# A kept TensorE order for one attention layer: later output products, transposes after the value projection, outputs in a projection bank

## The chip, the core and the metric

The kernel runs on one core of one Trainium2 chip. The metric is the device time of one execution in microseconds, as the median of several runs. Before the change the runs took 1037.28, 1037.68 and 1043.04 us; the median is 1037.68 us.

## What is computed

The reference is a decoder layer with three token mixers and a routed mixture of experts, followed by two layers of another design; 256 tokens of 1024 channels pass through all of them. Only the attention of the last layer is touched. Its core:

```python
def moba_attention(h, w_qkv, w_o):
    qkv = (h @ w_qkv).reshape(Bsz, S, 3, N_HEADS, HEAD_DIM)
    q = rope(q, pos) * (HEAD_DIM ** -0.5)
    k = rope(k, pos)
    ...
        s_own = jnp.where(kpos[None, :] <= qpos[:, None], s_own, NEG_INF)
        p = jax.nn.softmax(jnp.concatenate([s_sel, s_own], axis=-1), axis=-1)
    ...
    return o @ w_o
```

With 256 tokens there is a single block of 256 keys, so the selected blocks are all masked and what is left is causal attention of 16 heads of 64 channels over 256 positions, then the projection `w_o` and the residual. A gated feed-forward layer with a short convolution stands before it and another one after it.

## The kernel before

Weights arrive as 1 MB tiles of float32, and each is split into a high part in `float32r` (a ScalarE copy in `split`, L287) and a low part (a VectorE subtraction, L291), so that every product is made of three TensorE matmuls: high by high, high by low, low by high. `unit` (L467) is 48 such matmuls of 256 columns into one PSUM bank; `tm_unit` is the same for two banks with tokens on the partitions; `acc_rows` (L327) is 48 matmuls into four banks that are kept over all calls.

PSUM has eight banks in two rings of four: `bank` (projections: `un`, `pv`, and at the end the four output accumulators `wo`) and `abank` (attention: `sc` for scores, `ptT` for transposed weights, `po` for outputs). Splits rotate over three SBUF tiles, large tiles over eight.

The attention works on four blocks of four heads. For block j, `qkv(j, 0)` and `qkv(j, 1)` make queries and keys (`un`, 48 matmuls each) and rotate them: one VectorE product with the cosines, four on 32 partitions with the sines (`rb`), and a GpSimd addition (L1484). `qkv(j, 2)` makes the values (`pv`, 48 matmuls) and ScalarE evicts them. `scores(j)` makes 16 matmuls of float32 and 8 that add the causal mask, then two maxima for each head on VectorE (L1508, L1509), a scaling, two exponentials for each head on ScalarE with their sums, and one VectorE reciprocal (L1513). `weights(j)` multiplies by the reciprocals (one VectorE instruction over all heads for the first 128 queries, L1520, tile `pe`, and four ScalarE instructions), makes twelve transposes (L1526) into four banks and copies each bank to SBUF, on VectorE for even heads and on ScalarE for odd ones (tile `pT`). `values(j)` makes 16 matmuls into `po`, a ScalarE copy to the high part `oh` and a VectorE subtraction to the low part `ol`. The projection `acc_rows` of block j takes `oh` and `ol` of block j.

The loop at L1551 writes the stages in this order for j from 0 to 3: queries of j, scores of j-1, keys of j, weights of j-1, values projection of j, outputs of j-1. After it stand, for block 3, scores, projection 0, weights, projection 1, outputs, projection 2, and projection 3. This order is only a priority: a list scheduler that plans with a cost model of its own puts the instructions on each engine's queue, taking what it believes to be ready, earlier lines first. On the chip every queue then runs in the planned order. `chain` (L213) can fix that order for TensorE: while `chained[0]` is true, each instruction that `mm` or `flip` makes is ordered behind the one before. In the attention `chained[0]` is false, and the transposes at L1526 don't go through `flip`.

Of the kernel before, what the change touches and what calls it, by code (L numbers as in the profile page):

```python
# [21 lines left out]
P = 128  # L22
# [152 lines left out]
def build(tc, I, out, dbg=None, stop=None):  # L175
    nc = tc.nc
# [11 lines left out]
    def nm(s):  # L188
        uid[0] += 1
        return f"{s}_{uid[0]}"  # L190

    def big(n="b", dt=F32):
        return b8.tile([P, RAW], dt, tag="b8", name=nm(n))

    def mid(n="m", dt=F32, bufs=10):
        return sm.tile([P, 512], dt, tag="t512", name=nm(n), bufs=bufs)

    def tiny(n, w, dt=F32, bufs=2, p=P, tag=None):
        return sm.tile([p, w], dt, tag=tag or f"tn_{n}", name=nm(n), bufs=bufs)

    def bank(n="ps"):
        return ps.tile([P, 512], F32, tag="ps", name=nm(n), bufs=4)

    def abank(n="pa"):
        return ps.tile([P, 512], F32, tag="acc", name=nm(n), bufs=4)
# [5 lines left out]
    chained = [False, None]  # L211

    def chain(i):  # L213

        if chained[0]:
            if chained[1] is not None:
                behind(i, chained[1])
            chained[1] = i

    def mm(o, l, r, start, stop):  # L220
        chain(nc.tensor.matmul(o, l, r, start=start, stop=stop, skip_group_check=True))  # L221

    def flip(o, i):
        chain(nc.tensor.transpose(o, i, ident))
# [7 lines left out]
    def act(o, i, f, **kw):  # L232
        return S.activation(o, i, f, **kw)  # L233
# [20 lines left out]
    def tt(o, a, b, op):  # L254
        V.tensor_tensor(out=o, in0=a, in1=b, op=op)  # L255

    def ts(o, a, s1, op0, s2=None, op1=None):
        if s2 is None:
            V.tensor_scalar(out=o, in0=a, scalar1=s1, scalar2=None, op0=op0)
        else:  # L260
            V.tensor_scalar(out=o, in0=a, scalar1=s1, scalar2=s2, op0=op0, op1=op1)
# [10 lines left out]
    def ld(ap, n=RAW):  # L272
        t = raw.tile([P, RAW], F32, tag="raw", name=nm("raw"))
        nc.sync.dma_start(out=t[:, :n], in_=ap)
        return t
# [11 lines left out]
    def split(ap, n, on=None):  # L287

        hl = spl.tile([P, RAW], F32R, tag="spl", name=nm("spl"))
        hi, lo = hl[:, :PIECE], hl[:, PIECE:]  # L290
        queue(act(hi[:, :n], ap, AF.Copy), (on or V).tensor_tensor(out=lo[:, :n], in0=ap, in1=r32(hi[:, :n]), op=SUB))  # L291
        return hi, lo
# [34 lines left out]
    def acc_rows(t, xs, acc, first, last):  # L327

        w = [split(t[:, j * D:(j + 1) * D], D) for j in range(2)]
        for j, b in [(j, b) for b in range(KC) for j in range(2)] if last else [(j, b) for j in range(2) for b in range(KC)]:  # L330
            (hi, lo), (xh, xl) = w[j], xs[j]
            o = acc[b // 2][:, (b % 2) * T:(b % 2) * T + T]
            c = slice(b * P, b * P + P)
            mm(o, hi[:, c], xh, first and j == 0 and b % 2 == 0, False)
            mm(o, hi[:, c], xl, False, False)
            mm(o, lo[:, c], xh, False, last and j == 1)
# [27 lines left out]
    def C(name, p=P):  # L364
        return cst[:p, CST[name][0]:CST[name][1]]
# [7 lines left out]
    ident, ones = C("ident"), C("ones")  # L373
# [93 lines left out]
    def unit(src, xh, xl, on={}, order=range(KC)):  # L467

        p = bank("un")
        t = ld(src)  # L470
        cm_unit(t, P, 2, xh, xl, lambda b: (p[:, b * T:b * T + T], b == 0), on=on, order=order)
        return p
# [9 lines left out]
    def twice(rb):  # L482
        return rb.unsqueeze(1).to_broadcast([P, 2, T])
# [895 lines left out]
    def residual(x, acc):  # L1379
        for j in range(4):  # L1380
            s = slice(j * 512, j * 512 + 512)
            tt(x[:, s], x[:, s], acc[j], ADD)
# [87 lines left out]
    def qkv(j, i):  # L1470

        if i == 0:
            state[j] = [big("qkv")]
        g = state[j][0]
        if i < 2:
            p = pre.pop(0) if pre else unit(I["w_qkv"][3 * j + i], xh, xl)
            p3 = p.rearrange("p (h t) -> p h t", h=2)
            a, b_ = g[:, i * 512:i * 512 + 512], mid("rb")
            tt(a.rearrange("p (h t) -> p h t", h=2), p3, twice(cosr), MUL)
            for r in range(4):  # L1480
                src, dst = slice(32 * r, 32 * r + 32), slice(32 * (r ^ 1), 32 * (r ^ 1) + 32)
                tt(b_[dst].rearrange("p (h t) -> p h t", h=2), p3[src],
                   sinr[src].unsqueeze(1).to_broadcast([32, 2, T]), MUL)
            G.tensor_tensor(out=a, in0=a, in1=b_, op=ADD)  # L1484
            return
        t = ld(I["w_qkv"][3 * j + 2])
        pv = [bank("pv") for _ in range(2)]
        tm_unit(t, 256, KC, 0, xh, xl, pv, 7)
        for q in range(2):
            act(g[:, 1024 + q * T:1024 + q * T + T], pv[q][:, :T], AF.Copy, scale=rs[:, q:q + 1])  # L1490

    def scores(j):

        g = state[j][0]
        qr, kr = g[:, 0:512], g[:, 512:1024]
        pcs = [abank("sc") for _ in range(4)]
        for q in range(2):
            for h in range(4):
                s, o = slice(64 * (h % 2), 64 * (h % 2) + 64), (h // 2) * T
                mm(pcs[h][:, q * P:q * P + P + q * P], qr[s, o + q * P:o + q * P + P], kr[s, o:o + P + q * P], q == 0, False)  # L1500
        sums = tiny("sums", 8)
        pe = big("pe").rearrange("p (h t) -> p h t", h=4)
        for h in range(4):
            pc = pcs[h]
            mm(pc[:, 0:128], identb, nca, False, True)
            mm(pc[:, 256:384], identb, nca, False, True)
            m = tiny("amx", 2, bufs=4)
            V.tensor_reduce(out=m[:, 0:1], in_=pc[:, 0:128], axis=AX.X, op=MAX)  # L1508
            V.tensor_reduce(out=m[:, 1:2], in_=pc[:, 128:384], axis=AX.X, op=MAX)  # L1509
            ts(m, m, -0.125, MUL)  # L1510
            act(pe[:, h, 0:128], pc[:, 0:128], AF.Exp, scale=0.125, bias=m[:, 0:1], accum_out=sums[:, 2 * h:2 * h + 1])
            act(pe[:, h, 128:384], pc[:, 128:384], AF.Exp, scale=0.125, bias=m[:, 1:2], accum_out=sums[:, 2 * h + 1:2 * h + 2])
        V.reciprocal(sums, sums)  # L1513
        state[j] += [pe, sums]

    def weights(j):

        _, pe, sums = state[j]
        s2 = sums.rearrange("p (h q) -> p h q", q=2)
        tt(pe[:, :, 0:P], pe[:, :, 0:P], s2[:, :, 0:1].to_broadcast([P, 4, P]), MUL)  # L1520
        pTs = []
        for h in range(4):
            act(pe[:, h, P:3 * P], pe[:, h, P:3 * P], AF.Copy, scale=sums[:, 2 * h + 1:2 * h + 2])
            pt = abank("ptT")
            for b in range(3):
                nc.tensor.transpose(pt[:, b * P:b * P + P], pe[:, h, b * P:b * P + P], ident)  # L1526
            pT = mid("pT")
            if h % 2:
                act(pT[:, :384], pt[:, :384], AF.Copy)
            else:  # L1530
                V.tensor_copy(pT[:, :384], pt[:, :384])
            pTs.append(pT)
        state[j].append(pTs)

    def values(j):

        g, pTs = state[j][0], state[j][3]
        v = g[:, 1024:1536]
        po = abank("po")
        for r in range(2):  # L1540
            for i in range(2):
                h, o = 2 * r + i, po[64 * i:64 * i + 64, r * T:r * T + T]
                mm(o, v[:, 64 * h:64 * h + 64], pTs[h][:, 0:256], r == 0, False)
            for i in range(2):
                h, o = 2 * r + i, po[64 * i:64 * i + 64, r * T:r * T + T]
                mm(o[:, P:], v[:, T + 64 * h:T + 64 * h + 64], pTs[h][:, 256:384], False, True)
        s = slice(j * 512, j * 512 + 512)
        act(oh_[:, s], po, AF.Copy)
        tt(ol_[:, s], po, r32(oh_[:, s]), SUB)

    stages = (scores, weights, values)  # L1551
    for j in range(4):
        for i in range(3):
            qkv(j, i)
            if j:
                stages[i](j - 1)
    acc = [bank("wo") for _ in range(4)]
    for j in range(4):
        if j < 3:
            stages[j](3)  # L1560
        xs2 = [(oh_[:, (2 * j + b) * T:(2 * j + b + 1) * T], ol_[:, (2 * j + b) * T:(2 * j + b + 1) * T]) for b in range(2)]
        acc_rows(ld(I["w_ao"][j]), xs2, acc, j == 0, j == 3)
    residual(X, acc)
    dump("a1T", X)
    conv_ffn(1)
# [3 lines left out]
    po = [bank("fo") for _ in range(4)]  # L1569
# [54 lines left out]
```

## Time and profile before

| | us |
|---|---|
| median of three runs | 1037.68 |
| the profiled execution | 1044.24 |
| its span, first to last instruction | 1042.3 |
| TensorE busy | 984.4 |
| VectorE busy | 679.6 |
| ScalarE busy | 493.6 |
| GpSimd busy | 23.5 |

The first queries of the attention that stand inside the loop (block 1) start at 731.0 us of the span, and the last projection ends at 837.9 us. Times inside the span are counted from its first instruction. Busy time of TensorE counts a matmul that is overlapped by the next one, so a share of 94% says only that little idle time is visible. The granted clock is given as a share of the full 2.4 GHz.

### The profile page before, as it was taken

To read this page: it belongs to the slowest core of one execution; us is meant where nothing else is said; L and a number is where in the kernel's file an instruction comes from. 1 tells how busy PE (TensorE), PEld (TensorE's weight loads), DVE (VectorE), ACT (ScalarE), POOL (GpSimd) and SP (SyncE) were. 2 spreads that over 40 slices of the span, in tenths; PEclk is the share of its full clock that TensorE was granted. 3 is DMA by queue.
4 is the path that set the end of the run, shared out by engine and by line. 5 is a ranking of instruction groups with operands and counts; after the bars stand their busy time and mean duration, and the time that the engine had idled before them with its cause. 6 is when DMAs were issued, how large, how long until landed. Compare 5 with 4: busy or idle time off the path is not lost.

```text
span 1042.3 us, 18612 instructions
## 1 busy us (share of the span) xinstructions
PE 984.4 (94%) x7751; PEld 870.1 (83%) x7751; DVE 679.6 (65%) x1201; ACT 493.6 (47%) x776; POOL 23.5 (2%) x24
## 2 busy tenths in 40 slices
PE   6999997999989889999999999999899999999996
PEld 5988995555555439899999999999888999999996
DVE  5985554222233217885888777778987589777775
ACT  5646443222223226644555555555555556555554
POOL 0100000000000000100000000000211000000000
PEclk9999897999999999999999999999999999999998
DMA  8952355999999999555454545554333354544001
GB/s 327 419 222 79 122 221 219 417 380 420 420 420 389 420 416 420 191 172 193 163 190 174 195 170 200 168 199 172 122 122 122 133 192 163 199 165 163 1 1 41
DMA packets 35228, 232.45 MB, mean 223 GB/s; under 512 B 4288, under 2 KB 5056, under 8 KB 8640
## 3 DMA queue, kind: packets, MB, share of 16 engines
q1 hardware_dynamic: 34992, 231.14, 57.8%
q8 instruction: 67, 1.10, 0.4%
q14 instruction: 25, 0.20, 0.1%
q10 hardware_dynamic: 144, 0.02, 0.0%
HBM read 230.09 MB, written 1.05 MB: 222 GB/s over the span
## 4 chain that ended last, share of the span: by engine, by line
PE 53%; DMA 8%; DVE 7%; ACT 1%; issue 1%; POOL 0%; SPq 0%; DVEq 0%; ACTq 0%; POOLq 0%
PE un L221 35%; PE fo L221 11%; DMA mw<-in_w_dn_dram 3%; DMA mw<-in_w_gu_dram 3%; PE wo L221 2%; PE so L221 2%; DVE rb L255 2%; DVE spl L291 2%; DMA raw<-in_w_si_dram 1%; PE pv L221 1%; PE ptT L1526 1%; ACT spl L233 0%; PE po L221 0%; ACT pe L233 0%; PE ssq L221 0%
## 5 line engine op out<-in xcount | busy, mean ns | idle before, releaser
L221 PE MATMUL un<-nh,spl 128*128 128x256 f32 x2176 | 400.5, 284 | 2.8 <-DVE spl L291 2.6
L233 ACT ACTIVATE spl<-raw 128x1024 fp32r<-128x1024 f32 (+3 forms) x241 | 251.4, 1045 | 270.1 <-PE un L221 163.9
L291 DVE TENSOR_TENSOR spl<-raw,spl 128x1024 fp32r<-128x1024 f32 (+3 forms) x238 | 289.9, 1221 | 105.1 <-ACT spl L233 102.2
L221 PEld LDWEIGHTS un<-nh,spl 128*128 128x128 f32 x2176 | 342.9, 192 | 4.2 <-DVE spl L291 3.4
L221 PE MATMUL un<-nl,spl 128*128 128x256 f32 x1088 | 308.6, 284 | 1.9 <-DVE nl L264 1.9
L221 PEld LDWEIGHTS un<-nl,spl 128*128 128x128 f32 x1088 | 209.5, 193 | 2.3 <-DVE nl L264 2.3
L221 PE MATMUL fo<-ah,spl 128*128 128x256 f32 x704 | 130.1, 283 | 0.0
L221 PEld LDWEIGHTS fo<-ah,spl 128*128 128x128 f32 x704 | 111.2, 192 | 0.0
L221 PE MATMUL fo<-al,spl 128*128 128x256 f32 x352 | 99.8, 284 | 0.5 <-DVE al L255 0.4
L221 PE MATMUL pgu<-mw,xs 128*32 128x512 f32 x512 | 68.5, 621 | 8.2 <-DMA mw<-in_w_gu_dram 7.3
L1042 DVE COPY xs<-pgx 128x512 f32<-128x512 f32 x15 | 10.4, 691 | 100.1 <-PE pgx L221 100.1
L264 DVE SCALAR_TENSOR_TENSOR fc<-fz,vec,fc 128x254 f32<-128x254 f32 (+1 forms) x176 | 72.9, 477 | 1.4 <-ACT fc L233 1.4
L221 PEld LDWEIGHTS fo<-al,spl 128*128 128x128 f32 x352 | 67.5, 192 | 1.3 <-DVE al L255 1.3
L221 PEld LDWEIGHTS pgu<-mw,xs 128*32 128x32 f32 x512 | 17.3, 113 | 47.0 <-issue 30.6
L221 PEld LDWEIGHTS h<-pmT,yq 128*128 128x128 f32 x256 | 32.1, 190 | 20.5 <-issue 9.6
L233 ACT ACTIVATE su<-pgu,ws 128x512 f32<-128x512 f32 x8 | 5.5, 686 | 81.4 <-PE pgu L221 81.4
L221 PE MATMUL h<-pmT,yq 128*128 128x256 f32 x256 | 37.2, 292 | 7.2 <-DVE yq L264 3.8
L264 DVE SCALAR_TENSOR_TENSOR yq<-pd,ws,yq 128x512 fp32r<-128x512 f32 x32 | 22.9, 747 | 29.0 <-ACT yq L233 29.0
L255 DVE TENSOR_TENSOR fz<-un,rB 128x512 f32<-128x512 f32 x44 | 30.2, 690 | 16.1 <-PE un L221 16.0
L233 ACT ACTIVATE fc<-fz,vec 128x256 f32<-128x256 f32 x88 | 39.2, 496 | 1.1 <-DVE fz L255 1.1
L233 ACT ACTIVATE yq<-pd,ws 128x512 fp32r<-128x512 f32 x32 | 21.0, 685 | 37.7 <-PE pd L221 37.7
L221 PE MATMUL pd<-mw,sg 128*32 128x512 f32 x288 | 36.0, 596 | 1.1 <-DMA mw<-in_w_dn_dram 0.5
(330 smaller groups left out, 1363.8 us busy)
## 6 DMA issues: line engine op xcount, KB each, us to landing
mw<-in_w_gu_dram SPq DMA_DIRECT2D x64, 1024.0 KB, 15.0
raw<-in_w_fu_dram SPq DMA_DIRECT2D x44, 1024.0 KB, 4.7
mw<-in_w_dn_dram SPq DMA_DIRECT2D x28, 1024.0 KB, 12.5
raw<-in_w_fd_dram SPq DMA_DIRECT2D x22, 1024.0 KB, 4.7
raw<-in_w_si_dram SPq DMA_DIRECT2D x12, 1024.0 KB, 16.8
raw<-in_w_qkv_dram SPq DMA_DIRECT2D x12, 1024.0 KB, 4.7
raw<-in_w_o_dram SPq DMA_DIRECT2D x4, 1024.0 KB, 17.3
mw<-in_w_dn_dram SPq DMA_DIRECT2D x8, 512.0 KB, 14.4
```

The costliest lines, as they stand in the source:

```text
L221: chain(nc.tensor.matmul(o, l, r, start=start, stop=stop, skip_group_check=True))
L233: return S.activation(o, i, f, **kw)
L255: V.tensor_tensor(out=o, in0=a, in1=b, op=op)
L264: return V.scalar_tensor_tensor(out=o, in0=a, scalar=s, in1=b, op0=op0, op1=op1, **kw)
L291: queue(act(hi[:, :n], ap, AF.Copy), (on or V).tensor_tensor(out=lo[:, :n], in0=ap, in1=r32(hi[:, :n]), op=SUB))
L1042: V.tensor_copy(o, pg)
L1526: nc.tensor.transpose(pt[:, b * P:b * P + P], pe[:, h, b * P:b * P + P], ident)
```

## The change

The attention's TensorE instructions are chained, from the value projection of block 0 to the last projection, and the transposes go through `flip` so that they are in the chain. The order of stages is a new one: queries of block j, outputs of j-2, scores of j-1, keys of j, value projection of j, weights of j-1. After the loop stand scores of 3, outputs of 2, projections 0 and 1, weights of 3, projection 2, outputs of 3, projection 3. The tile `po` is taken from the ring `bank` for blocks 0 to 2, and from `abank` for block 3. No instruction is added or taken away on any engine.

```diff
-                nc.tensor.transpose(pt[:, b * P:b * P + P], pe[:, h, b * P:b * P + P], ident)
+                flip(pt[:, b * P:b * P + P], pe[:, h, b * P:b * P + P])
...
-        po = abank("po")
+        po = (abank if j == 3 else bank)("po")
...
-    stages = (scores, weights, values)
+    def at(f, j):
+        if 0 <= j < 4:
+            f(j)
+
+    chained[:] = [True, None]
     for j in range(4):
-        for i in range(3):
-            qkv(j, i)
-            if j:
-                stages[i](j - 1)
+        qkv(j, 0)
+        at(values, j - 2)
+        at(scores, j - 1)
+        qkv(j, 1)
+        qkv(j, 2)
+        at(weights, j - 1)
+    scores(3)
+    values(2)
     acc = [bank("wo") for _ in range(4)]
     for j in range(4):
-        if j < 3:
-            stages[j](3)
+        if j == 2:
+            weights(3)
+        if j == 3:
+            values(3)
         xs2 = [(oh_[:, (2 * j + b) * T:(2 * j + b + 1) * T], ol_[:, (2 * j + b) * T:(2 * j + b + 1) * T]) for b in range(2)]
         acc_rows(ld(I["w_ao"][j]), xs2, acc, j == 0, j == 3)
+    chained[:] = [False, None]
     residual(X, acc)
```

## Rows read from the trace of the kernel before

**Rows 1.** The page, busy time: engine, us, share of the span, instructions.

```profile
PE 984.4 (94%) x7751; PEld 870.1 (83%) x7751; DVE 679.6 (65%) x1201; ACT 493.6 (47%) x776; POOL 23.5 (2%) x24
```

**Rows 2.** Stretches: start:end, us, busy us by engine, granted clock, DMA share, GB/s.

```profile
731.00:757.73 26.73, 23.43 (x197) 21.47 (x197) 25.41 (x43) 14.99 (x33) 6.18 (x4) 1.00 0.32 119
757.73:783.87 26.14, 24.06 (x198) 22.69 (x197) 20.42 (x34) 13.35 (x32) 3.07 (x2) 0.93 0.36 126
783.87:808.39 24.52, 22.50 (x198) 21.23 (x196) 20.35 (x33) 13.23 (x32) 3.06 (x2) 1.00 0.33 125
808.39:837.89 29.50, 29.07 (x248) 27.69 (x247) 17.70 (x32) 15.86 (x38) 0.00 (x0) 1.00 0.40 143
```

**Rows 3.** The chain that ended last, attention: start, us, what it was.

```profile
756.35 1.45 PE po L221 x16
757.80 5.96 PE un L221 x48
```

**Rows 4.** TensorE in order of time: start, us, line, instructions [idle before <-releaser].

```profile
738.16 0.38 PE L221 MATMUL pv<-spl,nh 128*128 128x256 f32 x1 [0.91 <-ACT spl L233]
739.27 1.58 PE L221 MATMUL sc<-qkv 64*128 64x128 f32 x16 [0.73 <-POOL qkv L1484]
...
742.71 0.50 PE L221 MATMUL un<-nh,spl 128*128 128x256 f32 x2 [0.89 <-DVE spl L291]
...
763.68 0.49 PE L221 MATMUL sc<-qkv 64*128 64x128 f32 x4
...
765.62 0.36 PE L221 MATMUL un<-nh,spl 128*128 128x256 f32 x1
...
778.01 1.92 PE L1526 MATMUL ptT<-cst,pe 128*128 128x128 f32 x12 [2.08 <-DVE pe L255]
...
782.42 0.44 PE L221 MATMUL po<-pT,qkv 128*64 128x256 f32 x2
...
804.08 1.50 PE L1526 MATMUL ptT<-cst,pe 128*128 128x128 f32 x12 [2.02 <-DVE pe L255]
805.34 0.36 PE L221 MATMUL pv<-spl,nh 128*128 128x256 f32 x1
...
806.94 1.52 PE L221 MATMUL po<-pT,qkv 128*64 128x256 f32 x16
...
810.39 0.92 PE L221 MATMUL sc<-qkv 64*128 64x128 f32 x4 [0.43 <-DVE ol L255]
...
826.11 0.39 PE L221 MATMUL wo<-oh,spl 128*128 128x256 f32 x1
```

**Rows 5.** Stretches after the two waits of the transposes, columns as in group 2.

```profile
778.00:782.50 4.50, 4.49 (x26) 4.27 (x28) 4.24 (x4) 1.46 (x3) 1.00 (x1) 0.62 0.00 0
804.00:807.00 3.00, 2.92 (x26) 2.81 (x27) 2.97 (x3) 1.29 (x3) 1.07 (x1) 1.00 0.00 0
```

**Rows 6.** VectorE in order of time, columns as in group 4.

```profile
763.78 0.69 DVE L255 TENSOR_TENSOR qkv<-un,rope 128x512 f32<-128x512 f32 x1 [0.56 <-PE un L221]
...
777.17 0.69 DVE L255 TENSOR_TENSOR pe<-pe,sums 128x512 f32<-128x512 f32 x1
777.78 2.30 DVE L291 TENSOR_TENSOR spl<-raw,spl 128x1024 fp32r<-128x1024 f32 x1
780.12 1.02 DVE L1531 COPY pT<-ptT 128x384 f32<-128x384 f32 x2
...
803.86 2.30 DVE L291 TENSOR_TENSOR spl<-raw,spl 128x1024 fp32r<-128x1024 f32 x1
...
825.86 1.23 DVE L291 TENSOR_TENSOR spl<-raw,spl 128x1024 fp32r<-128x1024 f32 x1 [1.65 <-ACT spl L233]
827.00 0.68 DVE L255 TENSOR_TENSOR ol<-po,oh 128x512 fp32r<-128x512 f32 x1
```

**Rows 7.** GpSimd in order of time, columns as in group 4.

```profile
777.22 1.78 POOL L1484 TENSOR_TENSOR qkv<-qkv,rb 128x512 f32<-128x512 f32 x1 [8.43 <-DVE rb L255]
```

**Rows 8.** ScalarE in order of time: the copy of the last block's outputs.

```profile
826.23 0.60 ACT L233 ACTIVATE oh<-po 128x512 fp32r<-128x512 f32 x1 [0.41 <-PE po L221]
```

## The prediction

> **What bounds the kernel now.** The page comes first. TensorE is busy for 94% of the span and VectorE, the next one, for 65% [rows 1], so what the attention can give is TensorE's idle or slow time there, and not more. The stretches by block show how much that is. From the queries of block 1 to the end of the last projection there are four stretches of 26.73, 26.14, 24.52 and 29.50 us [rows 2], together 106.9 us. The work in them follows from the chain and the order of time: 48 matmuls of a projection 5.8 to 5.96 us, 16 output matmuls 1.45 [rows 3], 24 score matmuls from 763.68 to 765.62 = 1.94, twelve transposes from 804.08 to 805.34 = 1.26 [rows 4]. A block of the loop is then 3 x 5.87 + 1.94 + 1.26 + 1.45 = 22.3 us, and the last stretch 4 x 5.87 + 4.65 = 28.1. So 4.4 + 3.8 + 2.2 + 1.4 = 11.8 us of 106.9 are lost, and this is the ceiling of any new order: 1.1% of the kernel.
>
> The rows of TensorE say where they go. Twice the transposes wait for the VectorE multiplication `pe`: 2.08 us before 778.01 and 2.02 us before 804.08 [rows 4]. After the first wait the granted clock averages 0.62 over 4.5 us, after the second it stays at 1.00 [rows 5]; 24 matmuls take 778.01 to 782.42 = 4.41 us there and 804.08 to 806.94 = 2.86 us here [rows 4]. The fall to 1.2 GHz costs 1.55 us. Block 1 loses its time in small pieces, 0.91, 0.73 and 0.89 us [rows 4], while VectorE is busy for 25.41 of 26.73 us [rows 2]: VectorE sets that block. Before the scores of block 3, a bank that `po` holds costs 0.43 us [rows 4].
>
> **The change, part by part.** It adds no instruction and no DMA; it moves work on TensorE, and SP's and GpSimd's queues keep their order. In each of blocks 2 and 3 the planned order already was queries, scores, keys, 36 value matmuls, transposes, 12 value matmuls, outputs [rows 4]. So the change does two things: the 12 value matmuls (1.44 us) go ahead of the transposes, and the outputs (1.45 us) go behind the next queries, ahead of the scores.
>
> *Transposes of blocks 1 and 2.* What is late is VectorE's line of work from the end of the queries: it starts at 763.78 and ends with the multiplication at 777.17 + 0.69 = 777.86 [rows 6], 14.1 us. The new order puts `ol` of an older block (0.68 us [rows 6]) into that line: 14.8 us. TensorE's own work from the end of the queries to the end of the value projection becomes 1.45 + 1.94 + 5.87 + 5.87 = 15.1 us. VectorE is ready 0.3 us earlier, the hand-over takes 778.01 - 777.86 = 0.15 us, and both waits go but for some 0.2 us each: 2.08 + 2.02 - 0.4 = -3.7 us. The bounds: -4.1, and 0 if VectorE's order grows by another split or two. I take the middle line because all its pieces are rows; the margin is a few tenths only.
>
> *The clock.* It fell once behind two equal waits, so it is no sure consequence. With the wait that stood ahead of it gone, I take the fall as gone: -1.55. Bounds: -1.55 and +1.55 (one more).
>
> *Queries of block 3, directly behind transposes.* Their first low part was not needed before 783.87 [rows 2]; VectorE makes it right behind the multiplication, in 2.30 us, beside a GpSimd addition of 1.78 us [rows 6, 7]; the same split is 1.23 us without one [rows 6]. Transposes end 0.15 + 1.26 = 1.41 us behind the multiplication, two matmuls of 0.12 need only the high part, and the third waits for 2.30: about +0.65. Bounds: 0, and 1.9 with a split of 1.23 more ahead of it. In block 1 VectorE has its splits ready before.
>
> *Scores of block 3, directly behind transposes.* They need the four banks that the transposes just filled, and so the four copies `pT`. Before, 12 value matmuls and 16 output matmuls lay between. In both blocks that show it, VectorE runs a split of 2.30 us between multiplication and copies, and then two copies in 1.02 us [rows 6]. If that stays, the copies are done 3.3 us behind the multiplication, the transposes 1.4, and only the first two score matmuls fit between (0.2 us): +1.7 us. If the copies come first it is +0.4 (the last copy alone); with both splits of projection 0 ahead, +2.9. I take 1.7, since the rows show a split there. The 0.43 us of the `po` bank goes, as `po` now lies in the other ring: -0.43. That ring then holds queries, `po`, keys and two value banks in turn, five tenants on four banks, each evicted at least one projection (5.9 us) before its bank is needed again: nothing. If that cover went, the last eviction, `oh` and `ol`, would show: 0.60 + 0.68 [rows 6, 8].
>
> *Outputs of block 3, directly ahead of projection 3.* Before, projection 2 (5.9 us) lay between. Now the first matmul of projection 3 waits for `oh` and the second for `ol`. Before, the projection behind the outputs began at 826.11 [rows 4]; the copy ran 0.60 us from 826.23, and the subtraction of 0.68 us ended at 827.68, behind a split that ended at 827.09 [rows 6, 8]. With VectorE free the subtraction would end at about 827.5: +1.45 us. Bounds: 1.4, and 2.7 with a split of 1.23 in the way [rows 6].
>
> *Block 1.* The four value matmuls that ran in the gaps before the scores and behind them [rows 4] are no longer there to fill them: +0.5; transposes are no longer mixed with value matmuls one by one: -0.3. Together +0.2, bounds 0 and +0.5. The gaps themselves stay, as VectorE makes them.
>
> *Moved transposes and outputs of block 3.* They stand one projection later than before, so what they wait for has 5.9 us of cover more: nothing.
>
> The sum: -3.7 - 1.55 + 0.65 + 1.7 - 0.43 + 1.45 + 0.2 = -1.7 us. The profiled execution took 1044.24 us in all (span 1042.3), so the same execution would take 1042.5. The median of the runs is 6.6 us below the profiled one, and all three lie between 1037.28 and 1043.04; I carry the difference over to the median: 1037.68 - 1.7 = 1036.0 us. All terms at their good ends give -4.1 - 1.55 + 0.4 - 0.43 + 1.4 = -4.3 (1033.4); all at their bad ends, without a new fall of the clock, 0 + 0 + 1.9 + 2.9 - 0.43 + 2.7 + 0.5 = +7.6 (1045.3).
>
> **The rivals.** *New waits eat the rest (same time or a little longer).* The waits of the transposes shrink only by the 1.44 us that go ahead of them, since `ol` and splits lengthen VectorE's line: -2.9 instead of -3.7, the clock stays as it was, and the other terms stand: -2.9 + 3.6 = +0.7, 1038.4 us. For it: VectorE is busy for 20.4 of 26 us in these blocks [rows 2] and its line beats TensorE's by 0.3 us only. Against: every piece of the line has a row.
>
> *VectorE becomes the bound (slower).* Place: the VectorE queue ahead of the multiplication of blocks 1 and 2. If the planner puts the two splits of the next queries (2.30 + 1.23 us [rows 6]) ahead of it there, the transposes wait 3.5 us in each block, not 2.05: +2.9, and with the terms at the ends +3.6, the clock as before: +6.5, 1044.2 us. It decides from a wait of 0.3 us on: (4.1 - 3.6) / 2 is what the two waits may last until the gain is spent, clock left aside. Against it: multiplication stands ahead of the splits in the rows [rows 6], and the value projection gives it more time.
>
> *The clock falls more often (slower).* The new order has waits of 1.7, 1.45 and 0.65 us at places where there was none. If the clock falls behind the two longer ones as it did at 779, and the old fall stays, that is 3 x 1.55 in place of 1 x 1.55: from -1.7 to +2.95, so 1040.6 us. A rule stands on this side: the Trainium skill, "TensorE: Matmul & The Clock Gate", section "A second HAM failure mode: psum-queue depth-cycling", says that frequent short idle pieces between groups of matmuls make the clock go up and down, with a loss at each turn. The trace speaks against it here: block 1 has the most such pieces and a granted clock of 1.00 throughout [rows 2, 4].
>
> *All clean (faster).* Copies and splits fall well, every term at its good end: -4.3, 1033.4 us. Beyond that only the small pieces of block 1 could go; to gain over 1% (10.4 us) nearly all of the 11.8 us would have to.
>
> *The order changes nothing.* As the planned order is close to the new one, the sum could be within a few tenths of zero: 1037.7 us.
>
> **The numbers.** Forecast 0.40; new waits eat the rest 0.20; VectorE the bound 0.12; clock 0.08; all clean 0.13; nothing 0.07. From 1033.4 to 1040.6 lies most of it; the runs before spread over 5.8 us, so the range is 1031 to 1042. It leaves out 0.12 for VectorE as the bound and a little on the good side. A difference of under 1% (10.4 us) is what I can't tell from no change; the ceiling of 11.8 us makes faster 0.04, the worst sum of +7.6 makes slower 0.04, same 0.92.
>
> **What the profile after would show.** Right: the transposes of blocks 1 and 2 stand behind 48 value matmuls with waits under 0.5 us; no half clock near 779; a wait of the scores of block 3 on a `pT` copy, over 1 us; a wait of projection 3 on `oh` or `ol`, about 1.4 us; small waits of block 1 as before. Wrong: waits of the transposes over 1 us, or VectorE running splits ahead of `pe`; no wait at projection 3; a queue of VectorE or ScalarE ordered so differently that the feed-forward layer behind starts otherwise.

## The result: slower by 1.0%

The changed kernel takes 1048.39 us (median of 7 runs, 1047.62 to 1052.34), the kernel before 1037.68 (7 runs, 1035.71 to 1044.12): ratio 1.0103, 95% interval 1.0083 to 1.0122. The prediction said 1036.0 with a range of 1031 to 1042 and gave 0.04 to a loss of over 1%.

The profiled execution took 1048.39 us, with a span of 1046.5. The part ahead of the attention varies from execution to execution by some microseconds: the queries of block 1 begin at 731.00 us in the profile before and at 725.04 here, where the queues ahead are the same. So spans can't be compared, but stretches inside can. From the first queries of block 1 to the first matmul of the next layer the kernel before takes 731.00 to 837.73 = 106.7 us, the changed one 725.04 to 841.85 = 116.8 us: +10.1 us, close to the difference of the medians (10.7).

The stretches by block of the kernel after, from the queries of one block to those of the next, the last one from the scores of block 3 on; columns as in [rows 2]:

```profile
725.04:750.29 25.25, 22.64 (x181) 21.47 (x181) 23.96 (x41) 13.92 (x31) 6.91 (x4) 0.93 0.36 126
750.29:779.02 28.73, 25.19 (x199) 24.02 (x198) 22.47 (x35) 13.75 (x33) 3.88 (x3) 0.88 0.40 138
779.02:806.74 27.72, 24.11 (x199) 22.77 (x198) 20.90 (x34) 13.27 (x32) 3.62 (x2) 0.94 0.29 98
806.74:841.85 35.11, 32.09 (x262) 30.13 (x261) 18.01 (x33) 16.92 (x40) 0.00 (x0) 0.95 0.30 112
```

So one sees where the time went: the two middle blocks take 28.7 and 27.7 us for 22.3 us of work, and the clock is below 1.00 in every stretch, where it was below 1.00 in one [rows 2].

TensorE's longest waits in the same stretch of the kernel after (engine, line and what it waited for: us in total, times, longest):

```profile
PE pv L221 <- DVE spl L291: 7.2, 2, 3.6
PE wo L221 <- DVE ol L255: 2.3, 2, 1.8
PE sc L221 <- POOL qkv L1484: 2.3, 1, 2.3
PE wo L221 <- ACT oh L233: 0.7, 1, 0.7
```

The transposes don't stand in it any more. Their wait of 4.1 us has become 7.2 us of waiting in the middle of the value projection, for a low part of its weights. TensorE in order of time, kernel after (columns as in [rows 4]):

```profile
772.27 0.80 PE L221 MATMUL pv<-spl,nh 128*128 128x256 f32 x2 [3.54 <-DVE spl L291]
...
777.13 0.63 PE L224 MATMUL ptT<-cst,pe 128*128 128x128 f32 x2
...
801.07 0.38 PE L221 MATMUL pv<-spl,nh 128*128 128x256 f32 x1 [3.61 <-DVE spl L291]
...
814.94 0.39 PE L221 MATMUL wo<-oh,spl 128*128 128x256 f32 x1 [1.84 <-DVE ol L255]
...
835.25 0.39 PE L221 MATMUL wo<-oh,spl 128*128 128x256 f32 x1 [0.70 <-ACT oh L233]
836.11 0.38 PE L221 MATMUL wo<-ol,spl 128*128 128x256 f32 x1 [0.47 <-DVE ol L255]
```

What VectorE did meanwhile is the point. Kernel after, block 2:

```profile
766.55 0.20 DVE L1513 RECIPROCAL sums<-sums 128x8 f32<-128x8 f32 x1 [1.75 <-ACT pe L233]
766.86 0.69 DVE L255 TENSOR_TENSOR pe<-pe,sums 128x512 f32<-128x512 f32 x1
767.47 0.68 DVE L255 TENSOR_TENSOR qkv<-un,rope 128x512 f32<-128x512 f32 x1
768.17 2.79 DVE L255 TENSOR_TENSOR rb<-un,rope 32x512 f32<-32x512 f32 x4
770.99 4.58 DVE L291 TENSOR_TENSOR spl<-raw,spl 128x1024 fp32r<-128x1024 f32 x3
```

and the same place in the kernel before:

```profile
772.45 1.23 DVE L291 TENSOR_TENSOR spl<-raw,spl 128x1024 fp32r<-128x1024 f32 x1 [0.89 <-ACT spl L233]
773.59 0.20 DVE L1513 RECIPROCAL sums<-sums 128x8 f32<-128x8 f32 x1
773.70 0.64 DVE L255 TENSOR_TENSOR qkv<-un,rope 128x512 f32<-128x512 f32 x1
774.35 2.79 DVE L255 TENSOR_TENSOR rb<-un,rope 32x512 f32<-32x512 f32 x4
```

Before, the order was second split of the value weights, reciprocal, rotation, and the multiplication `pe` last [rows 6]. After, it is reciprocal, multiplication, rotation, and the split last. The multiplication, which the transposes used to wait for, ends at 767.55, some 3.8 us ahead of the time at which the value projection could have ended without a wait (765.45 + 5.87 = 771.32). The split, which TensorE now needs first, comes behind it. The high part of that split, which ScalarE makes, was ready at 767.47:

```profile
766.38 1.09 ACT L233 ACTIVATE spl<-raw 128x1024 fp32r<-128x1024 f32 x1
```

So it is VectorE's own order that holds the low part back, for 3.5 us.

The half clock (1.2 GHz, a granted clock of 0.50) follows the waits. Windows of the kernel after:

```profile
771.90:778.50 6.60, 6.23 (x29) 6.23 (x30) 4.15 (x4) 1.60 (x3) 1.45 (x1) 0.50 0.70 245
801.00:806.00 5.00, 4.93 (x29) 4.93 (x30) 3.60 (x4) 1.34 (x3) 1.17 (x1) 0.66 0.77 241
814.90:820.00 5.10, 5.06 (x29) 5.06 (x30) 1.23 (x1) 1.55 (x3) 0.00 (x0) 0.67 0.15 31
```

What is left of the value projection behind the wait, and the transposes, take 772.27 to 779.02 = 6.75 us and 801.07 to 806.74 = 5.67 us, against 3.97 us at full clock (run e1 below, 771.49 to 775.46): 2.8 and 1.7 us. The 78 matmuls behind the third wait take 814.94 to 825.89 = 10.95 us, 1.5 us more than at 11.59 us for 96 (run e3). Together 6.0 us.

The account: value projection +7.15, transposes -4.10, clock 6.0 in place of 1.55 (+4.45), the wait for a bank +1.84, projection 3 +1.17, scores of block 3 -0.8 (806.74 to 809.22 = 2.48, against 808.39 to 811.68 = 3.29 before, where the 0.43 us wait for a bank is part of it): +9.7 us. Measured are +10.1. The 0.4 us left fit what the rows of waits leave out at their ends: from the outputs of block 3 to the second matmul of projection 3 it is 833.04 to 836.11 = 3.07 us for 1.57 us of work, 1.50 us lost, where the two waits add up to 1.17.

### The profile page after: what moved, and what is told of

The parts are those of the page before. It is cut to its first block, busy times and chain, and to the rows that moved or that the text cites. A ratio compares the mean times of both kernels' runs of the same rounds, so it can differ in the third digit from the quotient of the medians.

```text
span 1046.5 us, 18609 instructions
## 1 busy us (share of the span) xinstructions
PE 983.5 (94%) x7751; PEld 871.2 (83%) x7751; DVE 681.0 (65%) x1201; ACT 493.5 (47%) x776; POOL 25.6 (2%) x24
## 4 chain that ended last, share of the span: by engine, by line
PE 53%; DVE 8%; ACT 2%; issue 1%; POOL 0%; DVEq 0%; ACTq 0%; POOLq 0%
PE un L221 34%; PE fo L221 11%; DVE spl L291 2%; PE so L221 2%; PE wo L221 2%; DVE rb L255 2%; PE pv L221 1%; ACT pe L233 1%; PE ptT L224 1%; ACT spl L233 0%; PE ssq L221 0%; PE rb L221 0%; DVE nl L264 0%; DVE qkv L255 0%; DVE fc L264 0%
```

## The experiments

Theory A after the two traces: the written order of stages makes the planner turn VectorE's queue round, and TensorE's kept order wants the old one; the longer waits then bring the clock down. The rival: the kept order is too tight or harmful in itself. The stretch named "attention" below goes from the first queries of block 1 to the first matmul of the next layer in each run's profile. The changed kernel, e1 to e4, e5 to e8, and e9 with e10 were each measured beside the kernel before in a set of their own (its medians: 1037.68, 1038.88, 1038.54, 1036.76 us), so a difference between medians of two sets can be off by some 2 us; the ratios are those within a set.

| run | median us | ratio to before, 95% interval | attention us |
|---|---|---|---|
| before | 1036.8 to 1038.9 in four sets | | 106.7 |
| after | 1048.39 | 1.0083 to 1.0122 | 116.8 |
| e1, rotation late | 1042.71 | 0.9979 to 1.0050 | 109.2 |
| e2, wait filled | 1045.41 | 1.0017 to 1.0088 | 112.8 |
| e3, outputs of block 2 first | 1045.19 | 1.0016 to 1.0080 | 112.8 |
| e4, block 3 early | 1047.81 | 1.0042 to 1.0103 | 112.8 |
| e5, mended | 1033.59 | 0.9926 to 0.9977 | 102.2 |
| e6, transposes late alone | 1045.08 | 1.0031 to 1.0081 | 112.7 |
| e7, outputs late alone | 1036.69 | 0.9952 to 1.0012 | 103.5 |
| e8, changed without chain | 1042.80 | 0.9998 to 1.0053 | 105.8 |
| e9, mended without chain | 1035.79 | 0.9966 to 1.0008 | 102.1 |
| e10, chain alone | 1051.74 | 1.0125 to 1.0172 | 118.5 |

### e1: the rotation of the keys written later

```diff
 def qkv(j, i):
-    (projection of keys, then their rotation)
+    (projection of keys; for j > 1 the rotation is written behind the value projection)
```

> The changed kernel, with one thing moved: in blocks 2 and 3 the rotation of the keys is written behind the value projection instead of ahead of it. TensorE's order stays the same; on VectorE the second low part of the value weights goes ahead of the four sine products of the keys, and nothing else on any queue changes place. Theory A (the waits of 3.54 and 3.61 us in the middle of the value projection come from VectorE's queue order, and the half clock behind them from the waits): both waits shrink to about 0.2 us, the falls of the clock behind them go (about 4.8 us), and new waits of 1.5 to 3.5 us appear where the next projection's split or the copies of the transposes now stand behind the rotation: in all 5 to 9 us below the changed kernel, 1040 to 1043 us. Theory B (the kept TensorE order is itself too tight, whatever stands on VectorE): the loss only moves, and the time stays within 2 us of 1048.4.

Measured: 1042.71 us, 5.7 below the changed kernel; attention 109.2 us, 7.6 less. VectorE in block 2 of this run:

```profile
769.01 0.69 DVE L255 TENSOR_TENSOR pe<-pe,sums 128x512 f32<-128x512 f32 x1
769.62 0.68 DVE L255 TENSOR_TENSOR qkv<-un,rope 128x512 f32<-128x512 f32 x1
770.22 1.22 DVE L291 TENSOR_TENSOR spl<-raw,spl 128x1024 fp32r<-128x1024 f32 x1
771.47 2.79 DVE L255 TENSOR_TENSOR rb<-un,rope 32x512 f32<-32x512 f32 x4
```

and TensorE's waits:

```profile
PE sc L221 <- DVE pT L1541: 2.7, 1, 2.7
...
PE pv L221 <- DVE spl L291: 1.3, 2, 0.7
```

The value projection of block 2 behind its wait, to the next queries:

```profile
771.49 0.51 PE L221 MATMUL pv<-spl,nh 128*128 128x256 f32 x2 [0.61 <-DVE spl L291]
...
775.46 0.36 PE L221 MATMUL un<-nh,spl 128*128 128x256 f32 x1
```

With TensorE's order untouched, one split ahead of four sine products takes the waits from 3.54 and 3.61 us to 0.61 and 0.69, and the falls of the clock behind them are gone: 3.97 us here, 6.75 in the changed kernel. The new first line is a wait at the place where the prediction had put one, the scores of block 3: 2.75 us for the copies of the transposes, which now stand behind the sine products and two splits. Theory A holds; the kept order itself has room.

### e2: the wait filled with work that nobody needs

```diff
-tm_unit(t, 256, KC, 0, xh, xl, pv, 7)
+tm_unit(t, 256, KC, 0, xh, xl, pv, 7, extra=24 if j > 1 else 0)   # 24 matmuls between its two halves
...
```

> The changed kernel with 24 extra matmuls of 256 columns in the middle of the value projections of blocks 2 and 3; they multiply data that is there already and write to the unused half of the projection's banks, so no result changes. They take 2.9 us each time and stand where TensorE waits 3.54 and 3.61 us. Theory A (the idle time brings the clock down and the half clock costs 4.8 us by itself): the waits shrink to 0.6 us, the clock stays up behind them, and the kernel is about 4 to 5 us faster, 1043 to 1045 us, though it does more work. Rival (the clock falls for another reason, or its loss is hidden by VectorE): within 1 us of 1048.4, or longer by the filler.

Measured: 1045.41 us, 3.0 below the changed kernel and 0.4 above the range of theory A; attention 4.0 us less, with 48 matmuls more. The intervals of the two overlap slightly, so it is the profile that carries this result. The waits are 0.66 and 0.73 us. The two stretches behind them:

```profile
773.70:778.00 4.30, 4.26 (x36) 4.26 (x37) 4.18 (x4) 1.69 (x4) 1.13 (x1) 1.00 0.67 244
799.70:804.00 4.30, 4.26 (x35) 4.10 (x36) 4.18 (x4) 1.69 (x4) 1.13 (x1) 1.00 0.67 244
```

The clock is 1.00 in both. VectorE delivers the split no earlier (21.98 us behind the queries of block 2 in both runs), so what is gained is the half clock by itself: 2.8 and 1.5 us, of which 0.4 is lost again at the scores of block 3 (2.87 us against 2.48). The Trainium skill, "TensorE: Matmul & The Clock Gate", section "HAM oscillation — how this bites in real kernels", describes a kernel whose clock falls while TensorE waits for its next operand, which there comes by DMA. Here it comes from VectorE, and this run agrees: with the idle time filled the clock is 1.00 in place of 0.50 and 0.66.

### e3: outputs of block 2 ahead of scores of block 3

```diff
-    scores(3)
     values(2)
+    scores(3)
```

> The changed kernel with outputs of block 2 ahead of scores of block 3. Theory A (projection 0 waits 1.84 us for the bank that the outputs of block 2 hold, because their eviction stands behind the softmax of block 3 on ScalarE and VectorE; the clock falls behind that wait for 1.75 us): the eviction comes before the softmax, the wait and the fall go, 0.5 us of waiting for the copies of the transposes comes ahead of the outputs: about 3 us faster, 1045.4 us. Rival (the bank is not what projection 0 waits for, or another wait takes its place): within 1 us of 1048.4.

Measured: 1045.19 us, attention 4.0 us less. `PE wo <- DVE ol` of 1.8 us is gone from the waits, and projections 0 and 1 run in one piece, 816.79 to 828.38. In the changed kernel the eviction of `po` stands behind the eight exponentials of block 3 on ScalarE and the multiplication on VectorE, and the fourth accumulator of the projection needs that bank. Changed kernel, the last exponential and the copy, then the subtraction:

```profile
812.72 0.50 ACT L233 ACTIVATE pe<-sc,amx 128x256 f32<-128x256 f32 x1
...
813.17 0.63 ACT L233 ACTIVATE oh<-po 128x512 fp32r<-128x512 f32 x1
...
814.20 0.68 DVE L255 TENSOR_TENSOR ol<-po,oh 128x512 fp32r<-128x512 f32 x1
```

Theory A holds.

### e4: weights and outputs of block 3 one projection earlier

```diff
-        if j == 2:
+        if j == 1:
             weights(3)
-        if j == 3:
+        if j == 2:
             values(3)
```

> The changed kernel with weights of block 3 ahead of projection 1 and outputs of block 3 ahead of projection 2, as the kernel before has them. Theory A (projection 3 waits 1.2 us for the copy and the subtraction of outputs that stand directly ahead of it): this wait goes, nothing else moves: 1.0 to 1.5 us faster, about 1047.2 us. Rival (transposes of block 3 one projection earlier now wait for their softmax): no gain, or up to 2 us longer.

Measured: 1047.81 us. The interval of this run and that of the changed kernel overlap, so the median settles nothing; the waits do. `PE wo <- ACT oh` (0.7) is gone and `PE wo <- DVE ol` is down from 2.3 to 1.8, the bank of e3. Those are the two waits of 1.17 us, which took 1.5 us in time. The rest of the 4.0 us by which its attention is shorter is mostly the clock: it didn't fall behind the 1.84 us wait in this execution (1.5 us), and block 2 lost 1.3 us less to it (779.22 to 784.68 = 5.5 us, against 6.75); the scores of block 3 give 0.4 back (2.87 us against 2.48).

### e5: all four moves

e1, e3 and e4 together, and on VectorE the low parts of projection 0's weights ordered behind the copies of the transposes of block 2 (`behind(low, copy)`), for the 2.7 us that e1 had left.

> The changed kernel with four moves: rotation of the keys behind the value projection (blocks 2 and 3), outputs of block 2 ahead of scores of block 3, weights and outputs of block 3 one projection earlier, and, on VectorE, the low parts of the first projection's weights behind the copies of the transposes of block 2. Theory A (each loss is a wait with its own cause on VectorE's queue, and they add): against the run with the late rotation the 2.75 us wait on the copies, the 1.84 us wait on the bank with its half clock, and the 1.2 us at projection 3 go; the attention then takes about 102 to 104 us instead of 106.9 before the change: 1033 to 1036 us. Theory B (the loss only moves): the time stays at 1040 us or above.

Measured: 1033.59 us, ratio 0.9952 (0.9926 to 0.9977): faster than both kernels. Its stretches:

```profile
723.33:748.57 25.24, 22.70 (x180) 21.39 (x181) 23.95 (x41) 13.92 (x31) 6.91 (x4) 0.93 0.35 125
748.57:771.59 23.02, 22.41 (x199) 21.23 (x198) 19.64 (x34) 13.02 (x32) 2.69 (x3) 1.00 0.39 137
771.59:794.85 23.26, 22.57 (x199) 21.23 (x197) 20.11 (x35) 13.24 (x32) 3.78 (x3) 1.00 0.39 137
794.85:825.53 30.68, 30.67 (x262) 28.26 (x261) 20.20 (x35) 16.61 (x40) 0.00 (x0) 1.00 0.39 138
```

Blocks 2 and 3 are within 1 us of the 22.3 us of work in them. Most of what is left stands in block 1, where VectorE is busy for 24 of 25 us. The losses had separate causes, and they add but for about 1 us: e1 took 7.6 us off the attention net of its new wait of 2.75, e3 4.0 and the waits of e4 1.2, together 15.5; e5 takes off 14.6.

### e6: one part alone, transposes behind the value projection

```diff
 (kernel before)  for each j
         qkv(j, 0);  scores(j - 1)
-        qkv(j, 1);  weights(j - 1);  qkv(j, 2);  values(j - 1)
+        qkv(j, 1);  qkv(j, 2);  weights(j - 1);  values(j - 1)
```

> The kernel before with one part of the change: weights behind the whole value projection instead of in the middle of it; no chain, no other move. VectorE's queue keeps its order. The prediction's first step as it stands: the waits of the transposes shrink from 2.05 to 0.6 us, but the outputs then stand directly behind the transposes and wait 1.4 to 1.9 us for the copies, which stand behind a split: no difference beyond 1 us, 1037 to 1040 us. Rival (this part brings the loss): 1044 us or more.

Measured: 1045.08 us: the rival was right on the time. TensorE's waits:

```profile
PE po L221 <- DVE pT L1531: 6.3, 3, 2.4
PE ptT L1526 <- DVE pe L255: 1.2, 2, 0.6
```

The transposes do wait 0.64 and 0.57 us, as forecast. But the outputs behind them wait 1.63, 2.35 and 2.35 us for the copies, the last two about 0.5 us more than I had reckoned, and the clock falls behind these two (a mean of 0.56 and 0.57 from 775.69 to 779.61 and from 803.55 to 807.38). The loss is not the changed kernel's: there the outputs stand a projection later.

### e7: the other part alone, outputs behind the next queries

```diff
 (kernel before)  for each j
         qkv(j, 0)
+        if j > 1:
+            values(j - 2)
         scores(j - 1);  qkv(j, 1);  weights(j - 1);  qkv(j, 2)
-        values(j - 1)
 ...
+    values(2)
```

and `po` in the projection ring, as in the change.

> The kernel before with the other part of the change: outputs of block j-2 behind the queries of block j and ahead of the scores of j-1, in a projection bank; no chain, weights where they were. Theory A (this part alone turns VectorE's queue round, since the planner then has the exponentials and the multiplication ready before the second split of the value weights): the second low part stands behind multiplication and rotation, the value projection waits about 3.5 us in blocks 2 and 3 and the clock falls behind: 1043 to 1048 us. Rival (the chain is what costs): within 1 us of the kernel before.

Measured: 1036.69 us, not slower than before. My theory fell. VectorE's queue did turn round in block 2 of this run:

```profile
768.22 0.69 DVE L255 TENSOR_TENSOR pe<-pe,sums 128x512 f32<-128x512 f32 x1
768.83 0.68 DVE L255 TENSOR_TENSOR qkv<-un,rope 128x512 f32<-128x512 f32 x1
769.52 2.79 DVE L255 TENSOR_TENSOR rb<-un,rope 32x512 f32<-32x512 f32 x4
772.35 1.02 DVE L1531 COPY pT<-ptT 128x384 f32<-128x384 f32 x2
773.40 2.51 DVE L291 TENSOR_TENSOR spl<-raw,spl 128x1024 fp32r<-128x1024 f32 x2
```

But TensorE isn't held to a written order here, and the planner put the transposes first there too:

```profile
766.92 0.28 PE L221 MATMUL pv<-spl,nl 128*128 128x256 f32 x1
769.05 0.88 PE L1526 MATMUL ptT<-cst,pe 128*128 128x128 f32 x6 [1.85 <-DVE pe L255]
```

Two value matmuls, then transposes, then the rest. With the multiplication early, transposes early are the order that fits. In block 3 VectorE kept the order of before: the split runs 791.72 to 792.95, the multiplication comes last, at 796.45, and the transposes stand behind 36 value matmuls:

```profile
797.29 1.50 PE L1526 MATMUL ptT<-cst,pe 128*128 128x128 f32 x12 [1.22 <-DVE pe L255]
```

So outputs late, with `po` in the other ring, turn VectorE's queue in one block of two. Transposes late alone (e6) turn it in none; both parts together turn it in both, with the chain and without (e8). Late outputs and the other ring weren't tried apart, and why the planner decides so isn't shown.

### e8: the changed kernel without the chain

```diff
-    chained[:] = [True, None]
```

> The changed kernel without the chain: the new written order is a priority only. VectorE's queue is the same but for the copies of the transposes. Theory A (the written order makes VectorE's queue, the chain on TensorE adds little): the value projection still waits for its second low part, but eleven transposes now stand in that wait and shorten it by 1.2 us each time: 1044 to 1048 us. Rival (the chain is the cause): 1037 to 1040 us.

Measured: 1042.80 us, between the two expectations: 1.2 us below the range of theory A, 2.8 above that of the rival. VectorE's queue is turned in blocks 2 and 3 as it is with the chain. The planner puts eleven of the twelve transposes into the wait:

```profile
772.18 1.36 PE L224 MATMUL ptT<-cst,pe 128*128 128x128 f32 x11
775.64 0.62 PE L221 MATMUL pv<-spl,nh 128*128 128x256 f32 x3 [2.09 <-DVE spl L291]
```

The waits are 2.09 and 2.17 us, the bank's wait is gone since the planner puts off the matmuls that need the bank, and the clock is at 1.00 from block 1 to the projections in the profile. The attention of the profile is 11 us shorter than with the chain. Of these, 1.1 us only move behind it: the next layer's first 96 matmuls take 834.71 to 847.31 = 12.6 us, against 841.85 to 853.37 = 11.5. The median is only 5.6 us lower. Falls of the clock behind the two waits in other executions would explain that; it isn't shown. So the turned queue without the chain leaves this profile about where the kernel before is. Most of the loss by the profiles, and half or more of it by the medians, needs the chain as well, which keeps the transposes out of the wait.

### e9: the mended kernel without the chain

> The mended kernel (late rotation, outputs of block 2 first, block 3 early, copies first) without the chain. Only TensorE's order in block 1 changes with it: four value matmuls go into the gap before and behind the scores of block 0. Theory A (where the written order and VectorE's queue fit, the chain does nothing): within 2 us of the mended kernel's 1033.6, at most shorter by the half clock behind the 2.25 us wait of block 1, 1.0 to 1.9 us. Rival (the mended kernel owes its time to the chain): 1036 us or more.

Measured: 1035.79 us, ratio 0.9987 (0.9966 to 1.0008); attention 102.1 us against 102.2 with the chain. The median lies between the two expectations, 0.2 us outside each. The profiles say that the chain gives nothing and costs nothing here. The medians leave it open: beside the kernel before of its own set the mended kernel gains 4.95 us with the chain and 0.97 without, and the two intervals overlap, so a gain of the chain of up to 4 us stays possible.

### e10: the chain alone

The kernel before, transposes through `flip`, `chained[0]` true over the attention; the written order is the old one.

> The kernel before with the chain and nothing else: the written order of stages stays, and TensorE has to keep it. VectorE's queue is the same as before. Theory A (the chain costs where the written order puts a product ahead of what VectorE can have ready): transposes now stand ahead of the whole value projection and wait from the end of the keys to the multiplication, about 6.4 us in blocks 2 and 3, with a fall of the clock behind each: 9 to 14 us slower than before, 1047 to 1053 us. Rival (the chain by itself is harmless): within 2 us of the kernel before.

Measured: 1051.74 us, ratio 1.0149, the slowest of all: inside the range of theory A, though 15.0 us above the kernel before of its set, where 9 to 14 were expected. The wait that decides:

```profile
PE ptT L224 <- DVE pe L255: 12.9, 3, 6.4
```

6.40 and 6.34 us ahead of the transposes of blocks 1 and 2, as worked out from the rows of before, and a granted clock of 0.51 and 0.50 behind them (775.5 to 779 and 806 to 809). What the planner did before, 36 value matmuls ahead of the transposes, was worth 4.3 us of waiting a block. A chain keeps whatever order is written, with every mistake in it.

## Where the prediction was right and where it was wrong

*What bounds the kernel.* Not contradicted: of the 11.8 us named as the ceiling of a gain e5 recovers 4.5. But a ceiling of the gain is no bound of the loss, and I let it narrow the whole range; the worst sum of +7.6 us held no fall of the clock, and it was the clock that carried the result past it.

*Transposes of blocks 1 and 2.* This is the step that failed. Its first half was right: no wait of the transposes over 0.2 us. The step took VectorE's line of work from the rows of before, added `ol`, and let the order inside stand; and it counted TensorE's way from the queries to the end of the value projection as 15.1 us of work without a wait, so that the projection's own weights stood nowhere in the sum. The written order is also the planner's priority, so a new one can be a new queue on every engine. Up to the multiplication the line was shorter than thought, 756.33 to 767.55 = 11.2 us in place of 14.8. But its last piece was now the second split of the value weights, for which TensorE waited until 772.27, 15.9 us from the line's start; and TensorE needs that split in the middle of the projection, at 768.7, not at its end. Waits of 3.54 and 3.61 us stood where none was forecast: with the 4.1 us that went, +3.05 us in place of -3.7, without the clock. The rival "VectorE becomes the bound" had the size, 3.5 us a block, and the engine, but the place wrong: it put splits ahead of the multiplication, and it was the multiplication and the rotation that stood ahead of the split. The signs of being wrong name the transposes and the splits ahead of `pe`, not the value projection.

*The clock.* Taken as gone, -1.55; measured 6.0 us in three falls behind waits of 3.54, 3.61 and 1.84 us. The rival with three falls gave 0.08 to this and priced each fall by one row, 1.55 us; they cost 2.8, 1.7 and 1.5. That it said three was luck: one of the three is in block 2, as it had it, but behind another wait, and the other two are not where it put them. A fourth fall, behind the first scores, cost nothing, as VectorE sets that block. And one trace was too few to set the rule on short idle pieces aside: the two waits ahead of the first scores, 0.91 and 0.73 us, for which the trace of before shows a clock of 1.00, are in e6, e7 and e9 too, and there it averages 0.52 behind them.

*The five tenants on four banks.* "Nothing" was wrong. I reckoned that each eviction has a projection ahead of it; for the last `po` it has the scores and the outputs only, and eight exponentials in the queue ahead. 1.84 us and a fall. The 0.43 us that went was right.

*Outputs of block 3 ahead of projection 3.* Forecast +1.45; measured waits of 0.70 + 0.47 = 1.17, in time 1.50. Right.

*Scores of block 3.* Forecast a wait of +1.7; measured no wait, and 2.48 us for 1.94 us of work. The copies came in time because the value projection was late: in e1, where it isn't, the scores wait 2.75 us for them, behind two splits as the step has it and behind the sine products that e1 moved. So the step was wrong in the changed kernel by the failure of the first one, and its mechanism is shown in e1 only in part.

*Queries of block 3.* Forecast +0.65, measured nothing: the splits stand in one row of three, and VectorE had done them at 775.57, ahead of the transposes.

*Block 1.* Forecast +0.2. From its queries to the scores of block 1 it is 725.04 to 757.67 = 32.6 us, and was 731.00 to 763.68 = 32.7. Right in the number, since VectorE sets that block; but the small waits became one of 2.25 us with half clock behind it.

## What to carry to other kernels

Where a planner makes the queues, a moved stage can change the order on other engines too, and the order on the engines that aren't the bound decides which wait comes next; a forecast that takes their order from the trace of before should price the other order too. Fix an order by hand on one engine only together with the order of the engines that feed it: e5 has the same TensorE order in the loop as the changed kernel and is 1.4% faster, by what stands on VectorE and by three moves at the end. And the price of a wait is not its length: the two waits of 3.6 us cost 2.8 and 1.7 us more at half clock.

## What was not expected of the hardware

The same wait brings the clock down in one execution and not in another. The 2.25 us wait ahead of the first scores was followed by half clock in the profiles of after, e1, e2, e3 and e5, and not in those of e4 and e10. Waits of 1.84 us at the same matmul were followed by it in after, e1 and e2, not in e4. Behind the 3.5 us waits of after, e3 and e4 it fell six times of six; behind 2.09 and 2.17 us in e8 not at all. Shorter waits can do it too. In the kernel before and in e6 to e9 the first scores stand behind two waits of 0.91 and 0.72 or 0.73 us with one matmul between them. They take 1.9 to 2.0 us at a clock of 1.00 in before and e8, and 3.5 to 3.6 us at a mean of 0.52 in e6, e7 and e9, here e7:

```profile
734.50 2.83 PE L221 MATMUL sc<-qkv 64*128 64x128 f32 x16 [0.72 <-POOL qkv L1484]
```

So single profiles with such waits differ by about 1.5 us a fall for this alone, where TensorE sets the pace (1.5 us behind the 1.84 us wait, 1.55 in the kernel before). Where VectorE does, a fall costs nothing: from its queries to the scores of block 1, block 1 takes 32.6 us after, with half clock in it, and in e4, without; and 32.2 us in e9 with it, 32.1 in e8 without.
